# A hybrid decoder layer on one core: weight splits moved to the highest scheduling priority, a triangular inverse dealt in two halves, and recurrence states rewritten with fewer VectorE operations

## The chip, the core and the metric

The kernel runs on one core of a Trainium2 chip. Its time is the device time of one execution in microseconds (us). Five engines work beside each other, each through its own instructions in order: TensorE (PE: matmuls, with its weight loads shown as PEld), VectorE (DVE), ScalarE (ACT), GpSimd (POOL) and SyncE (SP, which issues most of the transfers). An engine that waits for another holds everything that is queued behind the waiting instruction.

## What is computed

The reference is one residual layer. The input is normalised and multiplied by one wide matrix; four token mixers work on slices of that product; each mixer's output is gated, projected and merged, and an output projection is added to the input.

```python
h = rmsnorm(x, norm_gain)
proj = h @ w_in
ys = (gated_deltanet(...), spatial_gating(...), rwkv7_time_mix(...), native_sparse_attention(...))
gates = jnp.split(jax.nn.sigmoid(merge), N_MIXERS, axis=-1)
mixed = gates[0] * (ys[0] @ w_branch[0])
for i in range(1, N_MIXERS):
    mixed = mixed + gates[i] * (ys[i] @ w_branch[i])
x = x + mixed @ w_out
```

Two mixers are recurrences over the 1024 tokens: the gated DeltaNet (gdn) and RWKV-7. Both are worked in chunks of 32 tokens, in which the dependence inside a chunk is a unit lower triangular 32x32 system, and a state of 64x64 per head goes from chunk to chunk.

## The kernel before, in words

`body` first normalises x and splits it into a high and a low part (`hh`, `hl`, matmul type fp32r), so that a product of full precision is three matmuls. Then comes a row of **column tiles**: `col_tile(c, evac)` (L1008) loads 128 columns of the weight matrix in two halves (`load_w`, L997), splits each half into `wh` (a cast on ACT, L1004) and `wl` (a subtraction on DVE, L1006), and makes 48 matmuls of 512 columns in groups of three: `wh` with `hh` (L1017), `wl` with `hh` (L1018), `wh` with `hl` (L1019). `wt`, `wh` and `wl` have three buffers each, so a split can only run when the matmuls of an older half are done.

The order of the program text is: column tiles for RWKV; `rwkv`; column tiles for gdn; `gdn`; column tiles for the sparse attention (`nsa`) and `nsa` itself; the spatial mixer (`gmlp`); 32 column tiles for the merge gates; the branch products (L1250 to L1252) and the output projection (L1281 to L1284). The engines don't run it in this order. A scheduler takes all instructions and, with its own estimate of durations, hands them to the engines' queues; among those that it holds to be ready, the one earlier in the program text goes first. So column tiles written after a mixer fill the mixer's waiting times on PE, and their splits come behind the mixer's own DVE and ACT work. Each queue is fixed before the program runs.

`rwkv` and `gdn` go over four quarters of 256 tokens. A quarter is prepared (convolution or token shift, decays, products of keys; in gdn L465 is the convolution, L478 writes `KQ`, L480 the values), its eight triangular systems per four heads are inverted, and then eight steps of the recurrence run.

`unit_lower_inverse` (L81) inverts 32 systems of 32x32 at once on DVE. The rows of the inverse are dealt over four groups of 32 partitions: a partition holds 8 of the 32 rows of one system, rows 8g to 8g+7 for group g. `X` is (128, 8, 32). It walks from the last column pair to the first: for each of 16 values of c it multiplies all 8 rows by two columns of `L` (L98, 16 x m elements, m = 32-c) and sums the products (L100). The 32 instructions form one chain. Two transposes on PE (L103) and 16 copies (L110, L112) put the result where the recurrence needs it (`xt`).

A step of the recurrence is a chain over three engines. In rwkv: `py` (L312, L314) -> `R` (L319 DVE, L320 ACT) -> `px` (L322) -> `sv` (L323, L324) -> `ps` (L327) -> new state `S` by two DVE operations of 128x64 (L329), with `Sg`, the decayed old state, made ahead by L301. In gdn: `py` (L560) -> `R` by two DVE operations of 64x64 (L568) -> `px` of 64 columns (L572) -> `sa` (L573, L574) -> `ps` (L576) -> new state by two DVE operations of 128x64 (L578). L542, L544, L287 and L288 make the outputs of the step before.

Of the kernel before, what the change touches and what calls it, by code (L numbers as in the profile page):

```python
# [10 lines left out]
F32 = mybir.dt.float32  # L11
# [21 lines left out]
def setup(tc, ctx):  # L33
# [19 lines left out]
    for g in range(4):  # L53
        nc.gpsimd.iota(inv0[32 * g:32 * g + 32], pattern=[[-1, 8], [1, 32]], base=-8 * g, channel_multiplier=0,
                       allow_small_or_imprecise_dtypes=True)
# [25 lines left out]
def unit_lower_inverse(G, pool, src, xt):  # L81


    nc = G.nc
# [11 lines left out]
    for c in range(30, -1, -2):  # L96
        m = 32 - c
        nc.vector.tensor_mul(prv[:, :, :, :m], X[:, :, None, c:].to_broadcast([128, 8, 2, m]),  # L98
                             L[:, None, c:c + 2, c:].to_broadcast([128, 8, 2, m]))
        nc.vector.tensor_reduce(X[:, :, c:c + 2], prv[:, :, :, :m], axis=AX.X, op=OP.add)  # L100
# [3 lines left out]
    for r in range(4):  # L104
        for h in range(4):
            a = pt[32 * r:32 * r + 32, 0:256].rearrange("c (k g n h) -> c h n g k", k=2, g=4, h=4)[:, h]
            d = xt[32 * h:32 * h + 32, :, 32 * h:32 * h + 32]
            d = d.rearrange("c n (g k r) -> c r n g k", g=4, k=2)[:, r]
            if h % 2:
                nc.scalar.copy(d, a)  # L110
            else:
                nc.vector.tensor_copy(d, a)  # L112
# [11 lines left out]
def rwkv(G, src, zs, y, up, cols):  # L124
# [3 lines left out]
    with tc.tile_pool(name="rw", bufs=1, reuse_waits="tile") as P:  # L128
# [29 lines left out]
        for q in range(4):  # L158
# [136 lines left out]
            for n in range(8):  # L295
# [4 lines left out]
                Sg = P.tile([128, 2, 64], F32, name="Sg", bufs=2)  # L300
                nc.vector.tensor_mul(Sg, S, gdec[:, :, n:n + 1].to_broadcast([128, 2, 64]))  # L301
# [26 lines left out]
                for p in range(2):  # L328
                    nc.vector.scalar_tensor_tensor(S2[:, p], ps[:, 64 * p:64 * p + 64], gdec[:, p, n:n + 1],  # L329
                                                   Sg[:, p], op0=OP.mult, op1=OP.add)  # L330
# [29 lines left out]
def gdn(G, src, small, zs, y, conv, hp, gnw):  # L360
# [3 lines left out]
    with tc.tile_pool(name="gd", bufs=1, reuse_waits="tile") as P:  # L364
# [85 lines left out]
        for q in range(4):  # L450
# [102 lines left out]
            for n in range(8):  # L553
# [11 lines left out]
                R = P.tile([128, 64], F32, name="gR", bufs=2)  # L565
                for p in range(2):
                    hs = slice(64 * p, 64 * p + 64)
                    nc.vector.scalar_tensor_tensor(R[hs], py[hs, hs], egc[hs, 1, nn:nn + 1], V[hs, n],  # L568
                                                   op0=OP.mult, op1=OP.add)
                px = sbank(G)  # L570
                sa = SA[n % 2]
                nc.tensor.matmul(px[:, :64], xt[:, n], R, start=True, stop=True)  # L572
                nc.vector.tensor_scalar(sa[0:64, 0:64], px[0:64, :64], cn[0:64, 0, n:n + 1], None, op0=OP.mult)  # L573
                nc.scalar.activation(sa[64:128, 64:128], px[64:128, :64], AF.Copy, scale=cn[64:128, 0, n:n + 1])  # L574
                ps = sbank(G)
                nc.tensor.matmul(ps[:, :128], TB[:, n], sa, start=True, stop=True)  # L576
                for p in range(2):
                    nc.vector.scalar_tensor_tensor(S2[:, p], S[:, p], gl[:, p, nn:nn + 1],  # L578
                                                   ps[:, 64 * p:64 * p + 64], op0=OP.mult, op1=OP.add)
# [401 lines left out]
def body(tc, xT, x, w, wsm, rw_up, rw_cols, gd_conv, gd_hp, gd_gw, gm_ws, gm_bs, gm_lg, gm_lb,  # L981
# [4 lines left out]
    with ExitStack() as ctx:  # L986
# [22 lines left out]
        def col_tile(c, evac):  # L1009
            parts = [split_w(load_w(w[c], 4 * kh, 128), nc.vector) for kh in range(2)]  # L1010
# [356 lines left out]
```

## Time and profile before

| | us |
|---|---|
| median of 3 runs (1254.69 to 1255.78) | 1254.97 |
| the profiled execution | 1258.43 |
| span of its trace | 1256.7 |
| PE busy (94%), 6214 matmuls | 1185.8 |
| DVE busy (68%), 2181 instructions | 849.0 |
| ACT busy (41%) | 519.6 |
| POOL busy (14%) | 175.2 |

The profiled execution is 3.5 us longer than the median, and 1.7 us of it lie outside the span. Times in the trace count from the span's start. The rwkv recurrence runs from about 200 to 400 us, gdn from about 500 to 705, and from 1050 to the last tile PE has next to no waits. An operation's row gives the time from its start to its end; of instructions that follow each other the next can start before the end of the one before.

### The profile page before, as it was taken

To read this page: it belongs to the slowest core of one execution; us is meant where nothing else is said; L and a number is where in the kernel's file an instruction comes from. 1 tells how busy PE (TensorE), PEld (TensorE's weight loads), DVE (VectorE), ACT (ScalarE), POOL (GpSimd) and SP (SyncE) were. 2 spreads that over 40 slices of the span, in tenths; PEclk is the share of its full clock that TensorE was granted. 3 is DMA by queue.
4 is the path that set the end of the run, shared out by engine and by line. 5 is a ranking of instruction groups with operands and counts; after the bars stand their busy time and mean duration, and the time that the engine had idled before them with its cause. 6 is when DMAs were issued, how large, how long until landed. Compare 5 with 4: busy or idle time off the path is not lost. (4 is left out here: it accounts for less than half of the span.)

```text
span 1256.7 us, 17997 instructions
## 1 busy us (share of the span) xinstructions
PE 1185.8 (94%) x6214; PEld 962.6 (77%) x6214; DVE 849.0 (68%) x2181; ACT 519.6 (41%) x1302; POOL 175.2 (14%) x158
## 2 busy tenths in 40 slices
PE   6999999898999997998999999999999799999997
PEld 6987777786777785776777778787877577888886
DVE  6612697878774677878795579989876833588222
ACT  5422553361433355363533355645555343221212
POOL 4320000000002000010100000000000320576510
PEclk9999999998999998999999999999999999999999
DMA  5222453122211444212322422121114275676323
GB/s 196 101 93 101 134 149 103 45 70 67 98 59 59 112 149 121 98 61 81 115 75 85 162 94 76 64 76 56 59 47 145 100 238 186 214 236 217 110 84 126
DMA packets 113103, 140.09 MB, mean 111 GB/s; under 512 B 36544, under 2 KB 59968, under 8 KB 112884
## 3 DMA queue, kind: packets, MB, share of 16 engines
q1 hardware_dynamic: 95588, 107.22, 27.2%
q10 hardware_dynamic: 17424, 31.73, 6.6%
q8 instruction: 49, 0.80, 0.3%
q14 instruction: 42, 0.34, 0.1%
HBM read 94.78 MB, written 44.12 MB: 111 GB/s over the span
## 5 line engine op out<-in xcount | busy, mean ns | idle before, releaser
L1018 PE MATMUL st<-hh,wl 128*128 128x512 f32 x944 | 384.5, 407 | 9.4 <-DVE wl L1006 9.4
L1017 PE MATMUL st<-hh,wh 128*128 128x512 f32 x944 | 381.9, 406 | 3.2 <-ACT stg L1045 2.0
L1019 PE MATMUL st<-hl,wh 128*128 128x512 f32 x944 | 381.3, 404 | 0.0
L1018 PEld LDWEIGHTS st<-hh,wl 128*128 128x128 f32 x944 | 180.8, 192 | 44.0 <-DVE wl L1006 10.9
L1017 PEld LDWEIGHTS st<-hh,wh 128*128 128x128 f32 x944 | 180.2, 191 | 38.0 <-ACT stg L1045 3.5
L1019 PEld LDWEIGHTS st<-hl,wh 128*128 128x128 f32 x944 | 180.9, 192 | 32.3 <-issue 0.8
L1006 DVE TENSOR_TENSOR wl<-wt,wh 128x512 fp32r<-128x512 f32 x134 | 99.3, 744 | 94.2 <-ACT wh L1004 91.7
L1004 ACT CAST wh<-wt 128x512 fp32r<-128x512 f32 x140 | 86.4, 619 | 80.8 <-PE st L1019 66.5
L1045 ACT ACTIVATE stg<-st 128x512 f32<-128x512 f32 x64 | 38.2, 596 | 77.3 <-PE st L1019 76.9
L98 DVE TENSOR_TENSOR invP<-invX,invL 128x32 f32<-128x32 f32 (+15 forms) x128 | 55.7, 435 | 1.7
L100 DVE TENSOR_REDUCE invX<-invP 128x16 f32<-128x32 f32 (+15 forms) x128 | 54.9, 429 | 1.8
L915 ACT ACTIVATE P<-sc,m 128x512 f32<-128x512 f32 (+3 forms) x80 | 44.7, 564 | 25.3 <-DVE m L913 11.6
L1281 PE MATMUL sc<-woh,hh 128*128 128x512 f32 x128 | 49.8, 389 | 0.0
L1282 PE MATMUL sc<-wol,hh 128*128 128x512 f32 x128 | 49.8, 389 | 0.0
L1287 DVE TENSOR_TENSOR o<-sc,xr 128x512 f32<-128x512 f32 x16 | 11.1, 691 | 56.1 <-PE sc L1284 56.1
L1028 ACT COPY stg<-st 128x512 f32<-128x512 f32 x39 | 23.1, 591 | 61.0 <-PE st L1019 57.6
L1258 POOL TENSOR_TENSOR mx<-mx,stg 128x512 f32<-128x512 f32 x28 | 38.6, 1379 | 47.7 <-DVE stg L1257 46.6
L910 DVE TENSOR_REDUCE m<-sc 128x1 f32<-128x512 f32 (+3 forms) x80 | 40.7, 528 | 0.9 <-PE sc L835 0.3
L1264 ACT CAST hh<-mx 128x512 fp32r<-128x512 f32 x16 | 9.9, 621 | 62.6 <-POOL mx L1258 54.8
L30 POOL IOTA tril<- 128x128 f32 x1 | 0.2, 248 | 237.4 <-PE sc L835 237.4
L588 POOL TENSOR_TENSOR gst<-gst,mhalf 128x8 f32<-128x8 f32 x4 | 6.7, 1678 | 190.6 <-DVE gst L587 190.6
L254 POOL MEMSET sv<- 64x512 f32 x8 | 4.2, 519 | 207.8 <-ACT O L292 165.3
(457 smaller groups left out, 2400.7 us busy)
## 6 DMA issues: line engine op xcount, KB each, us to landing
wt<-in_w_dram SPq DMA_DIRECT2D x124, 256.0 KB, 2.7
gate<-stg ACTq DMA_DIRECT2D x64, 256.0 KB, 2.1
gt<-gate SPq DMA_DIRECT2D x32, 256.0 KB, 3.4
stg<-gate SPq DMA_DIRECT2D x32, 256.0 KB, 3.0
xt<-in_xT_dram SPq DMA_DIRECT2D x8, 512.0 KB, 5.0
wot<-in_wo_dram SPq DMA_DIRECT2D x16, 256.0 KB, 3.7
wt<-in_wb_dram SPq DMA_DIRECT2D x16, 256.0 KB, 3.5
xr<-in_x_dram SPq DMA_DIRECT2D x16, 256.0 KB, 2.5
```

The lines of the kernel that those rows point to most:

```text
L98: nc.vector.tensor_mul(prv[:, :, :, :m], X[:, :, None, c:].to_broadcast([128, 8, 2, m]), L[:, None, c:c + 2, c:].to_broadcast([128, 8, 2, m]))
L100: nc.vector.tensor_reduce(X[:, :, c:c + 2], prv[:, :, :, :m], axis=AX.X, op=OP.add)
L910: nc.vector.tensor_reduce(m2[:, h, gi:gi + 1], pz[:, :n], axis=AX.X, op=OP.max, negate=True)
L915: nc.scalar.activation(Pt[gi][:, h, :n], pp[gi][:, :n], AF.Exp, bias=m2[:, h, 0:1], accum_out=ss[:, gi, h:h + 1])
L1004: nc.scalar.copy(wh, wt)
L1006: eng.tensor_sub(wl, wt, wh.bitcast(F32))
L1017: nc.tensor.matmul(p, wh[:, kk], hh[:, k, sl], start=(k == 0), stop=False)
L1018: nc.tensor.matmul(p, wl[:, kk], hh[:, k, sl], start=False, stop=False)
L1019: nc.tensor.matmul(p, wh[:, kk], hl[:, k, sl], start=False, stop=(k == 7))
L1258: (nc.vector if j == 7 else nc.gpsimd).tensor_add(mx, mx, g)
L1281: nc.tensor.matmul(p, mh[:, k, ts], a[:, k], start=(k == 0), stop=False)
L1282: nc.tensor.matmul(p, mh[:, k, ts], b[:, k], start=False, stop=False)
```

## The change

1. `col_tile` puts the two instructions of a split (cast on ACT, subtraction on DVE) under `tc.high_priority()`: whenever the scheduler holds them to be ready, they go before anything else. The load of the weights stays where it was.
2. `unit_lower_inverse` deals the rows in turn (row 4r+g in place r of group g), so that all groups have the same number of rows that are not yet known to be zero; for a given c only rows from r0 = c//4 on are worked, in two halves of rows with an instruction each. There are 60 instructions in place of 32, and 3,120 products and as many sums per partition in place of 4,352 (the sum of rows x 2 x m over all c).
3. rwkv: the new state is (`ps` + S) times the decay: an addition and a multiplication of 128x128, in place of `Sg` and the two operations of L329.
4. gdn: `Sg` (the decayed state) is made ahead by two ACT operations of 128x64; `R` is one DVE operation of 128x128 with both head pairs (the halves that are not needed come along); `px` has 128 columns in place of 64; the new state is one addition of 128x128.

```diff
 setup:
-        nc.gpsimd.iota(inv0[32 * g:32 * g + 32], pattern=[[-1, 8], [1, 32]], base=-8 * g, ...
+        nc.gpsimd.iota(inv0[32 * g:32 * g + 32], pattern=[[-4, 8], [1, 32]], base=-g, ...
 unit_lower_inverse:
     for c in range(30, -1, -2):
-        m = 32 - c
-        nc.vector.tensor_mul(prv[:, :, :, :m], X[:, :, None, c:].to_broadcast([128, 8, 2, m]),
-                             L[:, None, c:c + 2, c:].to_broadcast([128, 8, 2, m]))
-        nc.vector.tensor_reduce(X[:, :, c:c + 2], prv[:, :, :, :m], axis=AX.X, op=OP.add)
+        m, r0 = 32 - c, c // 4
+        halves = [slice(r0, (r0 + 8) // 2), slice((r0 + 8) // 2, 8)] if r0 < 7 else [slice(7, 8)]
+        for rs in halves:
+            d = [128, rs.stop - rs.start, 2, m]
+            nc.vector.tensor_mul(prv[:, rs, :, :m], X[:, rs, None, c:].to_broadcast(d),
+                                 L[:, None, c:c + 2, c:].to_broadcast(d))
+        for rs in halves:
+            nc.vector.tensor_reduce(X[:, rs, c:c + 2], prv[:, rs, :, :m], axis=AX.X, op=OP.add)
 rwkv:
-                Sg = P.tile([128, 2, 64], F32, name="Sg", bufs=2)
-                nc.vector.tensor_mul(Sg, S, gdec[:, :, n:n + 1].to_broadcast([128, 2, 64]))
...
-                for p in range(2):
-                    nc.vector.scalar_tensor_tensor(S2[:, p], ps[:, 64 * p:64 * p + 64], gdec[:, p, n:n + 1],
-                                                   Sg[:, p], op0=OP.mult, op1=OP.add)
+                Su = P.tile([128, 2, 64], F32, name="Sg", bufs=2)
+                nc.vector.tensor_add(Su, ps[:, 0:128].rearrange("q (p e) -> q p e", p=2), S)
+                nc.vector.tensor_mul(S2, Su, gdec[:, :, n:n + 1].to_broadcast([128, 2, 64]))
 gdn:
-                R = P.tile([128, 64], F32, name="gR", bufs=2)
+                Sg = P.tile([128, 2, 64], F32, name="gSg", bufs=2)
                 for p in range(2):
-                    hs = slice(64 * p, 64 * p + 64)
-                    nc.vector.scalar_tensor_tensor(R[hs], py[hs, hs], egc[hs, 1, nn:nn + 1], V[hs, n],
-                                                   op0=OP.mult, op1=OP.add)
+                    nc.scalar.activation(Sg[:, p], S[:, p], AF.Copy, scale=gl[:, p, nn:nn + 1])
+                R = P.tile([128, 2, 64], F32, name="gR", bufs=2)
+                nc.vector.scalar_tensor_tensor(R, py[:, :128].rearrange("q (p e) -> q p e", p=2), egc[:, 1, nn:nn + 1],
+                                               V[:, n, None, :].to_broadcast([128, 2, 64]), op0=OP.mult, op1=OP.add)
-                nc.tensor.matmul(px[:, :64], xt[:, n], R, start=True, stop=True)
+                nc.tensor.matmul(px[:, :128], xt[:, n], R.rearrange("q p e -> q (p e)"), start=True, stop=True)
-                for p in range(2):
-                    nc.vector.scalar_tensor_tensor(S2[:, p], S[:, p], gl[:, p, nn:nn + 1],
-                                                   ps[:, 64 * p:64 * p + 64], op0=OP.mult, op1=OP.add)
+                nc.vector.tensor_add(S2, ps[:, :128].rearrange("q (p e) -> q p e", p=2), Sg)
 col_tile:
-            parts = [split_w(load_w(w[c], 4 * kh, 128), nc.vector) for kh in range(2)]
+            parts = []
+            for kh in range(2):
+                wt = load_w(w[c], 4 * kh, 128)
+                with tc.high_priority():
+                    parts.append(split_w(wt, nc.vector))
```

The scheduler makes a new order of all queues from this. The first place is DVE's queue in gdn, in the second half of the first quarter's inverse (`invP` is the product, `invX` the inverse, `cvt` the convolution of a later quarter, `stg` a gate's evacuation). Before:

```order
L100 TENSOR_REDUCE invX<-invP 128x8x2
L465 SCALAR_TENSOR_TENSOR cvt<-graw,cw,cvt 128x256
L98 TENSOR_TENSOR invP<-invX,invL 128x16x24
L465 SCALAR_TENSOR_TENSOR cvt<-graw,cw,cvt 128x256
L100 TENSOR_REDUCE invX<-invP 128x8x2
L1038 SCALAR_TENSOR_TENSOR stg<-stg 128x512
L98 TENSOR_TENSOR invP<-invX,invL 128x16x26
L1038 SCALAR_TENSOR_TENSOR stg<-stg 128x512
L100 TENSOR_REDUCE invX<-invP 128x8x2
L480 SCALAR_TENSOR_TENSOR cvt<-gth,cvt 128x512
L98 TENSOR_TENSOR invP<-invX,invL 128x16x28
L1006 TENSOR_TENSOR wl<-wt,wh 128x512
```

With the change, at the same part of the inverse (L102 is the product, L105 the sum, L1008 the subtraction of a split):

```order
L102 TENSOR_TENSOR invP<-invX,invL 128x6x18
L102 TENSOR_TENSOR invP<-invX,invL 128x6x26
L105 TENSOR_REDUCE invX<-invP 128x3x2 x2
L1008 TENSOR_TENSOR wl<-wt,wh 128x512
L102 TENSOR_TENSOR invP<-invX,invL 128x6x20
L102 TENSOR_TENSOR invP<-invX,invL 128x6x28
L105 TENSOR_REDUCE invX<-invP 128x3x2 x2
L102 TENSOR_TENSOR invP<-invX,invL 128x6x22
L102 TENSOR_TENSOR invP<-invX,invL 128x8x30
L105 TENSOR_REDUCE invX<-invP 128x3x2
L105 TENSOR_REDUCE invX<-invP 128x4x2
L102 TENSOR_TENSOR invP<-invX,invL 128x6x24
```

Before, every instruction of the inverse has a convolution or another operation of other work behind it, and the split's `wl` comes after all of the convolution; now the inverse's two halves follow each other, a `wl` stands between them, and the third quarter's convolution starts only at the inverse's last steps.

The second place is PE's queue from the `ps` of one step of gdn to the `px` of the next (last quarter). Before (L576 is `ps`, L560 `py`, L572 `px`):

```order
L576 MATMUL sc<-gSA_3539,gTB 128x128
L1019 MATMUL st<-hl,wh 128x512
L1017 MATMUL st<-hh,wh 128x512
L1018 MATMUL st<-hh,wl 128x512
L1019 MATMUL st<-hl,wh 128x512
L560 MATMUL sc<-gS,KQ_3536 128x128
L542 MATMUL sc<-gS,KQ_3536 128x128
L544 MATMUL sc<-gSA_3539,gKK 128x128
L1017 MATMUL st<-hh,wh 128x512
L1018 MATMUL st<-hh,wl 128x512
L572 MATMUL sc<-gR,gXT_3538 128x64
```

With the change (L580 is `ps`, L563 `py`, L576 `px`, L1023 to L1025 the column tiles):

```order
L580 MATMUL sc<-gSA_3619,gTB 128x128
L1023 MATMUL st<-hh,wh 128x512
L1024 MATMUL st<-hh,wl 128x512
L1025 MATMUL st<-hl,wh 128x512
L563 MATMUL sc<-gS,KQ_3616 128x128
L545 MATMUL sc<-gS,KQ_3616 128x128
L547 MATMUL sc<-gSA_3619,gKK 128x128
L1023 MATMUL st<-hh,wh 128x512
L576 MATMUL sc<-gR,gXT_3618 128x128
```

Of column matmuls, four stood between `ps` and `py` and now three; two stood before `px` and now one. Those taken out stand further back in the queue.

## Rows read from the trace of the kernel before

**Rows 1.** gdn's stretch: busy us (count) of PE, PEld, DVE, ACT, POOL; PE's clock; DMA.

```profile
500.00:725.00 225.00, 210.59 (x1085) 166.13 (x1085) 166.35 (x499) 95.18 (x270) 11.35 (x11) 0.96 0.31 101
```

**Rows 2.** Waits of PE: who for whom, us in total, times, longest us.

```profile
PE st L1018 <- DVE wl L1006: 9.4, 3, 7.6
PE m L272 <- DVE AR L251: 7.0, 3, 3.6
PE m L681 <- DVE gmv L674: 4.7, 1, 4.7
PE m L488 <- DVE KQ L478: 4.4, 3, 2.1
```

**Rows 3.** Timeline, 479 to 506 us, of PE: start us, us, instruction [idle before].

```profile
479.84 1.97 PE L525 MATMUL m<-KQ 128*64 128x128 f32 x32
...
500.87 0.80 PE L1018 MATMUL st<-hh,wl 128*128 128x512 f32 x1 [7.65 <-DVE wl L1006]
...
505.73 0.63 PE L103 MATMUL sc<-ident,invX 128*128 128x128 f32 x2
```

**Rows 4.** Timeline of ACT: the cast of the same split.

```profile
492.55 0.63 ACT L1004 CAST wh<-wt 128x512 fp32r<-128x512 f32 x1
```

**Rows 5.** Timeline of DVE: the split's subtraction, start and end of the inverse.

```profile
480.85 0.18 DVE L98 TENSOR_TENSOR invP<-invX,invL 128x32 f32<-128x32 f32 x1
...
500.13 0.68 DVE L1006 TENSOR_TENSOR wl<-wt,wh 128x512 fp32r<-128x512 f32 x1
...
504.44 0.69 DVE L100 TENSOR_REDUCE invX<-invP 128x16 f32<-128x512 f32 x1
```

**Rows 6.** Stretch behind that wait, columns as in rows 1.

```profile
500.80:506.40 5.60, 5.53 (x15) 4.36 (x16) 4.26 (x9) 0.01 (x1) 0.00 (x0) 0.50 0.86 282
```

**Rows 7.** Page, groups: line, operation, count | busy us, mean ns | idle before.

```profile
L98 DVE TENSOR_TENSOR invP<-invX,invL 128x32 f32<-128x32 f32 (+15 forms) x128 | 55.7, 435 | 1.7
L100 DVE TENSOR_REDUCE invX<-invP 128x16 f32<-128x32 f32 (+15 forms) x128 | 54.9, 429 | 1.8
```

**Rows 8.** Groups by shape of the inverse's product, widest and narrowest.

```profile
L98 DVE TENSOR_TENSOR invP<-invX,invL 128x512 f32<-128x512 f32 x8 | 5.5, 689 | 0.2
...
L98 DVE TENSOR_TENSOR invP<-invX,invL 128x32 f32<-128x32 f32 x8 | 1.5, 185 | 0.1
```

**Rows 9.** Timeline of DVE: two operations that don't depend on each other.

```profile
485.09 0.32 DVE L98 TENSOR_TENSOR invP<-invX,invL 128x160 f32<-128x160 f32 x1
485.33 0.48 DVE L465 SCALAR_TENSOR_TENSOR cvt<-graw,cw,cvt 128x256 f32<-128x256 f32 x1
```

**Rows 10.** Groups by shape: the state operations, and one of 128x128 out of PSUM.

```profile
L568 DVE SCALAR_TENSOR_TENSOR gR<-sc,egc,gV 64x64 f32<-64x64 f32 x64 | 18.1, 283 | 8.3 <-PE sc L560 7.1
L907 DVE TENSOR_TENSOR sc<-sc,ndg 128x128 f32<-128x128 f32 x64 | 17.7, 293 | 8.4 <-PE sc L835 8.1
L329 DVE SCALAR_TENSOR_TENSOR S<-sc,gdec,Sg 128x64 f32<-128x64 f32 x64 | 15.2, 279 | 14.9 <-PE sc L327 14.5
L578 DVE SCALAR_TENSOR_TENSOR gS<-gS,gl,sc 128x64 f32<-128x64 f32 x64 | 15.0, 275 | 11.5 <-PE sc L576 11.3
L301 DVE TENSOR_TENSOR Sg<-S,gdec 128x128 f32<-128x128 f32 x32 | 9.2, 288 | 0.4
```

**Rows 11.** Groups: PE's matmuls of 64 and of 128 columns in gdn.

```profile
L560 PE MATMUL sc<-gS,KQ 128*128 128x128 f32 x64 | 13.3, 292 | 1.6 <-DVE gS L578 1.6
L572 PE MATMUL sc<-gR,gXT 128*128 128x64 f32 x64 | 12.4, 276 | 2.9 <-ACT gXT L110 2.5 <-DVE gR L568 0.3
```

**Rows 12.** Timeline of PE: 128-column matmuls back to back.

```profile
855.34 0.27 PE L946 MATMUL m<-ident,P 128*128 128x128 f32 x1
855.45 0.27 PE L946 MATMUL sc<-ident,P 128*128 128x128 f32 x1
```

**Rows 13.** Groups: ACT's widest operation in a step of gdn.

```profile
L547 ACT ACTIVATE gO<-sc,egc 128x128 f32<-128x128 f32 x32 | 11.7, 367 | 38.7 <-PE sc L544 38.5
```

**Rows 14.** Timeline of DVE: where `wl` held the queue in gdn's preparation.

```profile
453.32 0.69 DVE L1006 TENSOR_TENSOR wl<-wt,wh 128x512 fp32r<-128x512 f32 x1 [4.81 <-ACT wh L1004]
...
476.86 0.69 DVE L1006 TENSOR_TENSOR wl<-wt,wh 128x512 fp32r<-128x512 f32 x1 [5.00 <-ACT wh L1004]
```

More of the change, by code (lines that the diff above doesn't have):

```diff
@@ L53, in setup @@
     for g in range(4):
-        nc.gpsimd.iota(inv0[32 * g:32 * g + 32], pattern=[[-1, 8], [1, 32]], base=-8 * g, channel_multiplier=0,
+        nc.gpsimd.iota(inv0[32 * g:32 * g + 32], pattern=[[-4, 8], [1, 32]], base=-g, channel_multiplier=0,
                        allow_small_or_imprecise_dtypes=True)
@@ L107, in unit_lower_inverse @@
             d = xt[32 * h:32 * h + 32, :, 32 * h:32 * h + 32]
-            d = d.rearrange("c n (g k r) -> c r n g k", g=4, k=2)[:, r]
+            d = d.rearrange("c n (k r g) -> c r n g k", g=4, k=2)[:, r]
             if h % 2:
@@ L564, in gdn @@
                         last = outputs(n - 1, S0, sa)
-                R = P.tile([128, 64], F32, name="gR", bufs=2)
+                Sg = P.tile([128, 2, 64], F32, name="gSg", bufs=2)
                 for p in range(2):
-                    hs = slice(64 * p, 64 * p + 64)
-                    nc.vector.scalar_tensor_tensor(R[hs], py[hs, hs], egc[hs, 1, nn:nn + 1], V[hs, n],
-                                                   op0=OP.mult, op1=OP.add)
+                    nc.scalar.activation(Sg[:, p], S[:, p], AF.Copy, scale=gl[:, p, nn:nn + 1])
+                R = P.tile([128, 2, 64], F32, name="gR", bufs=2)
+                nc.vector.scalar_tensor_tensor(R, py[:, :128].rearrange("q (p e) -> q p e", p=2), egc[:, 1, nn:nn + 1],
+                                               V[:, n, None, :].to_broadcast([128, 2, 64]), op0=OP.mult, op1=OP.add)
                 px = sbank(G)
                 sa = SA[n % 2]
-                nc.tensor.matmul(px[:, :64], xt[:, n], R, start=True, stop=True)
-                nc.vector.tensor_scalar(sa[0:64, 0:64], px[0:64, :64], cn[0:64, 0, n:n + 1], None, op0=OP.mult)
-                nc.scalar.activation(sa[64:128, 64:128], px[64:128, :64], AF.Copy, scale=cn[64:128, 0, n:n + 1])
+                nc.tensor.matmul(px[:, :128], xt[:, n], R.rearrange("q p e -> q (p e)"), start=True, stop=True)
+                nc.vector.tensor_scalar(sa[0:64, 0:64], px[0:64, 0:64], cn[0:64, 0, n:n + 1], None, op0=OP.mult)
+                nc.scalar.activation(sa[64:128, 64:128], px[64:128, 64:128], AF.Copy, scale=cn[64:128, 0, n:n + 1])
                 ps = sbank(G)
                 nc.tensor.matmul(ps[:, :128], TB[:, n], sa, start=True, stop=True)
-                for p in range(2):
-                    nc.vector.scalar_tensor_tensor(S2[:, p], S[:, p], gl[:, p, nn:nn + 1],
-                                                   ps[:, 64 * p:64 * p + 64], op0=OP.mult, op1=OP.add)
+                nc.vector.tensor_add(S2, ps[:, :128].rearrange("q (p e) -> q p e", p=2), Sg)
                 S0, S = S, S2
```

## The prediction

> **What bounds the kernel now.** I read the page first, then the waits of PE, then the timeline around the longest of them, then the groups that price the edited instructions. The page shows PE busy for 94% of the span, so the kernel ends when PE has worked off its queue; time can only be won where PE stands still, runs at the lower clock, or does less. No edit takes a matmul away. So the question is which of PE's waits the change removes, and what it puts in their place.
>
> The waits of PE [rows 2] are few and short, and those I list all end with a DVE result: 9.4 us for the low part of a weight split, 7.0 for the inputs of rwkv's chunk products (L272), 4.7 for gmlp's normalised values (L681), 4.4 for gdn's keys (L488). In gdn's stretch [rows 1] DVE is busy for 166 of 225 us, and PE's granted clock is 0.96 on average. The clock has two levels, 1.2 and 2.4 GHz, so 0.96 means that about 8% of the stretch, 18 us, ran at the lower one; work done there takes twice as long, so some 9 us are lost.
>
> One wait makes up most of the 9.4 us. At 500.87 PE starts a column matmul after 7.65 us of idling [rows 3]; it waited for a `wl` that DVE began at 500.13 [rows 5]. The cast that `wl` needs had ended at 492.55 + 0.63 = 493.18 [rows 4]. The subtraction was late only because of its place in DVE's queue, behind convolutions and the inverse, as the first excerpt of the order shows. Behind the wait PE ran 5.6 us at the lower clock, granted clock 0.50 [rows 6].
>
> **The splits at the highest priority, with the inverse: -10 us.** The priority alone would give almost nothing here. The next thing that PE needs is the inverse, at L103. The inverse's last sum ends at 504.44 + 0.69 = 505.13 [rows 5], and PE started L103 at 505.73 [rows 3]. Without the wait on `wl` PE would stand at L103 instead, and 0.6 us would be won. That is the lower end. But the order now also keeps the convolution out of the inverse. Before, 32 instructions took from 480.85 to 505.13, 24.3 us [rows 5], while their own durations sum to (55.7 + 54.9) / 8 = 13.8 us [rows 7].
>
> The new inverse: a product of 512 elements takes 689 ns and one of 32 takes 185 [rows 8], which is 1.05 ns an element and 151 ns fixed. 60 instructions over 6,240 elements are 60 x 0.151 + 6,240 x 0.00105 = 9.1 + 6.6 = 15.6 us, if each waits for the end of the one before. Of two operations that don't depend on each other the second begins earlier: one that began at 485.09 and took 0.32, to 485.41, was followed at 485.33 [rows 9], 0.08 us before its end. The two halves don't depend on each other at once, so up to 60 x 0.08 = 4.8 us go: 10.8 us. From 480.85, with two `wl` of 0.68 between, the inverse ends between 493 and 498.
>
> PE took from 479.84 to 505.73 between L525 and L103 [rows 3]. Less 7.65 of waiting, and less half of the 5.6 us at the lower clock (2.8), it would come to L103 at 495.3, 10.4 us earlier. It then waits 0 to 2.8 us for the inverse. I take a gain of 9, as the order shows the halves paired almost throughout. The other two waits for `wl` are 9.4 - 7.65 = 1.75 us together; I take 1 of it. Ends of this term: -0.6 and -12.2.
>
> **A lighter DVE: -8 us.** The inverse gives DVE 13.8 - 10.8 = 3.0 us in each of 8 quarters, 24 us. In gdn a step's `R` costs 18.1 / 32 = 0.57 us and the state 15.0 / 32 = 0.47 [rows 10]. One operation of 128x128 out of PSUM takes 0.29, the row of L907 [rows 10]; `R` becomes one (up to 0.35, being one with a scalar and two inputs: 0.279 for 64 elements plus 64 x 1.05 ns), the state the other. That is 0.4 us a step, 12.7 in all. In rwkv the pair takes 15.2 / 32 = 0.475 and `Sg` 0.288; now an addition (0.293) and a multiplication (0.288) do it [rows 10], 0.18 us a step, 5.8 in all. DVE gets some 42 us back, all in the stages where PE waits for it. The waits it could shorten are 7.0 + 4.7 + 4.4 = 16.1 us [rows 2]. I take half, since the new order also lets PE arrive earlier at such places: the second excerpt has fewer column matmuls in a step. Ends: 0 and -16.1.
>
> **Work that is added.** `px` in gdn has 64 more columns in 64 passes. The group of 128 columns is busy 13.3 us against 12.4 for 64 columns [rows 11], +0.9; passes of 128 columns follow each other by 0.11 us [rows 12], and half of that for 64 passes is +3.5. I take +2. In rwkv the chain grows, as the multiplication must follow the addition: 0.293 + 0.288 against 0.475 is +0.106 us a step, 3.4 in all. Column matmuls in the step cover it in most steps; I take +1, ends 0 and +3.4. gdn's 64 new ACT operations cost at most 64 x 0.367 = 23.5 us of ACT [rows 13], which is busy 95 of 225 us there [rows 1]. They need only the old state and lie beside `py` and `R`; if they came in front of ACT's half of `sa`, up to all of it would go into the chain. I cost them at nothing. The shorter chain of gdn, 0.4 us a step less the wider `px`, I cost at nothing as well: the scheduler took column matmuls out of the step to fit, and PE does them later. The dealing of rows moves only patterns of `iota` and copies, in equal numbers.
>
> **Sum.** -10 - 8 + 2 + 1 = -15 us on the profiled execution of 1258.4, so 1243.4; that execution stands 3.5 us above the median, and on the median of 1255 it is **1240**. The forecast's own range is 1228 (every gain at its end, -27) to 1250 (a third of the sum).
>
> **Rivals.**
>
> *The wait only moves* (chance 0.13). PE leaves the split's wait and stands at the inverse, or at the recurrence's next result. For it: the inverse ended only 0.6 us before PE came [rows 3, 5]. Against it: the convolution has left the inverse. Then -0.6 + 3, and a quarter of the second term (-4): -1.6, 1253.
>
> *The splits hold DVE's queue* (0.14, slower). A split ahead of everything is handed out as soon as a buffer is expected to be free; where PE is late, the cast waits for PE, `wl` for the cast, and everything on DVE behind it. This happens already: `wl` held DVE for 4.81 and 5.00 us in gdn's preparation [rows 14], the second time right ahead of the inverse. If each of the 8 inverses gets one more such hold of 4.9 us and half reaches PE, +20; with -10 + 3 that is +13, 1268. It decides for slower once more than 15 us of new holds reach PE. Against it: in the same trace the casts were done well before their `wl` where DVE was full [rows 4, 5].
>
> *Twice the instructions* (0.06, slower). If the halves don't overlap, an inverse takes 15.6 us and not 13.8, the first term gives 7, the other seven inverses come 1.8 us later, 12.5, and the second term is gone: +8.5, 1263. Rows 9 speak against it, with their 0.08 us. The Trainium skill, VectorE: DVE Perf Modes, in The DRAIN you can't avoid and Rules for kernel authors, says that after each operation the next can't start until the pipe is empty, so the count of operations is to be kept small; by that rule the halves win nothing, and the time would be this rival's. The same page adds that an instruction that isn't held starts earlier; the trace agrees with that part.
>
> *More than the sum* (0.13). Every listed wait goes (-28) and, with fewer waits, half of the 9 us lost to the clock in gdn comes back: -32, 1223.
>
> The forecast keeps 0.54. About 0.2% (2.5 us) is what a measurement of this kernel can tell from no change. Faster than that: 0.54 + 0.13 = 0.67; within: 0.13; slower: 0.20. The range of 1221 to 1262 takes in the larger gain and the moved wait, and leaves out the queue's holds and little else.
>
> **What would show it.** Right: no wait of PE on `wl` above 2 us near 490 to 510; the inverse groups sum to about 125 us of durations, but a first gdn inverse lasts under 17 us from first to last; L103 is reached some 9 us earlier; granted clock in gdn above 0.96. Wrong: new waits of PE at L103, `px` or `py` of 5 us and more; idle time of DVE ahead of `wl` with the inverse behind it; inverse operations that follow each other by their full duration.

## The result, and the profile after

| | us, median (lowest to highest) | span of the profiled execution | mean granted clock |
|---|---|---|---|
| before, in the same runs | 1255.89 (1254.69 to 1257.62) | 1256.7 | 0.977 |
| with the change | 1226.2 (1225.36 to 1229.06) | 1223.6 | 0.995 |

The ratio is 0.9768, with a 95% interval of 0.9755 to 0.9781. The change gains 29.7 us. The forecast of 1240 had the direction, and its range of 1221 to 1262 holds the time, but the gain is twice the 15 us that it expected.

First the page of the changed kernel: busy time of each engine, share of the span and number of instructions, and the three column matmuls of a split (line, operation, count | busy us, mean ns | idle just before).

```profile
PE 1168.8 (96%) x6214; PEld 948.3 (78%) x6214; DVE 816.5 (67%) x2309; ACT 539.0 (44%) x1366; POOL 176.8 (14%) x158
...
L1023 PE MATMUL st<-hh,wh 128*128 128x512 f32 x944 | 380.4, 403 | 2.3 <-ACT stg L1051 2.3
L1024 PE MATMUL st<-hh,wl 128*128 128x512 f32 x944 | 379.4, 402 | 0.0
L1025 PE MATMUL st<-hl,wh 128*128 128x512 f32 x944 | 377.2, 400 | 0.0
```

PE executes the same 6214 matmuls. Its busy time fell from 1185.8 us (94% of 1256.7) to 1168.8, by 17.0, and the rest of its span from 70.9 to 54.8, by 16.1. Of the 33.1 us between the two profiled spans, half is thus PE standing still less, and half is PE taking less time over the same work. The second half is the clock. With two levels of 1.2 and 2.4 GHz, a mean of 0.977 says that 4.6% of the span, some 58 us, ran at the lower one; 0.995 leaves some 12 us. L1024, the matmul that reads `wl`, waits for nothing now; before it stood 9.4 us [rows 2].

The waits of PE, with the columns of rows 2:

```profile
PE st L1117 <- ACT wh L1006: 6.5, 1, 6.5
PE m L491 <- DVE KQ L481: 4.4, 3, 2.2
PE sc L108 <- DVE invX L105: 4.3, 4, 1.8
PE m L683 <- DVE gmv L676: 3.6, 2, 1.9
```

The first is the program's start and stood in the kernel before with the same 6.5 us. No wait is above 2.2 us besides. `KQ` is unchanged from rows 2, `gmv` is 1.1 less, and the wait for `AR` of 7.0 has left the head of the list. The wait for the inverse at L108 is new, 4.3 us in four pieces.

Busy time by stretch, with the columns of rows 1: rwkv, gdn's preparation and gdn's recurrence. First the two stretches before that rows 1 leave out, then all three with the change.

```profile
200.00:425.00 225.00, 209.46 (x1167) 171.55 (x1165) 158.91 (x481) 86.79 (x261) 15.79 (x19) 0.96 0.25 75
425.00:500.00 75.00, 66.41 (x345) 52.24 (x345) 57.08 (x145) 40.96 (x133) 4.58 (x3) 0.95 0.38 114
```

```profile
200.00:425.00 225.00, 212.99 (x1220) 172.46 (x1219) 162.94 (x561) 92.96 (x270) 15.55 (x19) 1.00 0.25 74
425.00:500.00 75.00, 72.96 (x404) 58.45 (x403) 59.64 (x202) 45.98 (x153) 4.27 (x3) 1.00 0.46 145
500.00:725.00 225.00, 214.81 (x1275) 171.65 (x1274) 166.12 (x588) 121.90 (x365) 11.42 (x11) 0.99 0.31 100
```

In the last stretch PE starts 1275 matmuls where it started 1085 [rows 1], at a clock of 0.99 in place of 0.96. VectorE is as busy there as it was, 166 us: what the edits save is filled with work that used to come later.

What PE loses in a stretch can be estimated from these rows: its idle time, plus the length times what the clock lacks to 1.00. Before, that is 15.5 + 0.04 x 225 = 24.5 us in rwkv, 8.6 + 0.05 x 75 = 12.4 in gdn's preparation and 14.4 + 0.04 x 225 = 23.4 in its recurrence. With the change it is 12.0, 2.0 and 12.4. The rows give the clock in hundredths, which leaves each long stretch open by 1 us. By this estimate some 12 us of the gain lie in rwkv, 10 in the preparation and 11 in gdn's recurrence.

The first inverse of gdn on the timeline, of VectorE first and then of PE (start us, us, instruction):

```profile
459.32 0.34 DVE L102 TENSOR_TENSOR invP<-invX,invL 128x4 f32<-128x4 f32 x3
...
467.05 0.69 DVE L1008 TENSOR_TENSOR wl<-wt,wh 128x512 fp32r<-128x512 f32 x1 [0.58 <-ACT wh L1006]
...
475.71 0.42 DVE L105 TENSOR_REDUCE invX<-invP 128x8 f32<-128x256 f32 x1
```

```profile
463.72 1.97 PE L528 MATMUL m<-KQ 128*64 128x128 f32 x32
...
475.99 0.39 PE L1025 MATMUL st<-hl,wh 128*128 128x512 f32 x1
476.21 0.30 PE L108 MATMUL sc<-ident,invX 128*128 128x128 f32 x1
```

The inverse lasts from 459.32 to 476.13, 16.8 us against 24.3 [rows 5]. Two `wl` stand inside it. The one shown follows its cast at once, for which it held the queue 0.58 us; before, the `wl` that PE waited for came 7 us after its cast [rows 4, 5]. PE runs column matmuls back to back until the inverse is there, and needs 12.5 us from L528 to L108, with 44 column matmuls between, where it took 25.9 from L525 to L103 [rows 3], with 55.

### The profile page after: what moved, and what is told of

It is laid out like the page before. It is cut to its first block, busy times and chain, and to the rows that moved or that the text cites. A ratio compares the mean times of both kernels' runs of the same rounds, so it can differ in the third digit from the quotient of the medians.

```text
span 1223.6 us, 18178 instructions
## 1 busy us (share of the span) xinstructions
PE 1168.8 (96%) x6214; PEld 948.3 (78%) x6214; DVE 816.5 (67%) x2309; ACT 539.0 (44%) x1366; POOL 176.8 (14%) x158
## 5 line engine op out<-in xcount | busy, mean ns | idle before, releaser
L1023 PE MATMUL st<-hh,wh 128*128 128x512 f32 x944 | 380.4, 403 | 2.3 <-ACT stg L1051 2.3
L1024 PE MATMUL st<-hh,wl 128*128 128x512 f32 x944 | 379.4, 402 | 0.0
L1025 PE MATMUL st<-hl,wh 128*128 128x512 f32 x944 | 377.2, 400 | 0.0
L1023 PEld LDWEIGHTS st<-hh,wh 128*128 128x128 f32 x944 | 178.7, 189 | 35.9 <-ACT stg L1051 3.6
L1025 PEld LDWEIGHTS st<-hl,wh 128*128 128x128 f32 x944 | 178.4, 189 | 32.7 <-issue 1.0
L1024 PEld LDWEIGHTS st<-hh,wl 128*128 128x128 f32 x944 | 178.5, 189 | 32.3 <-issue 1.9
L1008 DVE TENSOR_TENSOR wl<-wt,wh 128x512 fp32r<-128x512 f32 x134 | 99.0, 740 | 96.4 <-ACT wh L1006 94.3
L102 DVE TENSOR_TENSOR invP<-invX,invL 128x16 f32<-128x16 f32 (+18 forms) x240 | 53.9, 259 | 0.3
L105 DVE TENSOR_REDUCE invX<-invP 128x8 f32<-128x240 f32 (+18 forms) x240 | 52.7, 252 | 0.2
L1293 DVE TENSOR_TENSOR o<-sc,xr 128x512 f32<-128x512 f32 x16 | 11.1, 692 | 56.1 <-PE sc L1290 56.1
L1270 ACT CAST hh<-mx 128x512 fp32r<-128x512 f32 x16 | 9.9, 622 | 62.6 <-POOL mx L1264 54.8
L1295 ACT ACTIVATE jk<-o 128x512 f32<-128x512 f32 x16 | 10.1, 631 | 51.6 <-DVE o L1293 51.6
```

Of the source, the lines that this page charges most:

```text
L102: nc.vector.tensor_mul(prv[:, rs, :, :m], X[:, rs, None, c:].to_broadcast(d), L[:, None, c:c + 2, c:].to_broadcast(d))
L105: nc.vector.tensor_reduce(X[:, rs, c:c + 2], prv[:, rs, :, :m], axis=AX.X, op=OP.add)
L1023: nc.tensor.matmul(p, wh[:, kk], hh[:, k, sl], start=(k == 0), stop=False)
L1024: nc.tensor.matmul(p, wl[:, kk], hh[:, k, sl], start=False, stop=False)
L1025: nc.tensor.matmul(p, wh[:, kk], hl[:, k, sl], start=False, stop=(k == 7))
```

## The experiments

Each kernel was timed in turn with the kernel before on the same chip; ratios are to that one. In all of them the computation is the reference's, in full.

**The parts alone.** The priority alone: only `col_tile` is changed.

```diff
-            parts = [split_w(load_w(w[c], 4 * kh, 128), nc.vector) for kh in range(2)]
+            parts = []
+            for kh in range(2):
+                wt = load_w(w[c], 4 * kh, 128)
+                with tc.high_priority():
+                    parts.append(split_w(wt, nc.vector))
```

> The kernel before with the highest priority for the weight splits alone. Theory (priority and inverse need each other): PE's 7.65 us wait on wl near 500 goes, but PE then stands at L103 for the inverse, so little is won there; 1250 to 1256 us. Rival 1 (the priority alone is the gain, as PE always has column matmuls at hand): 1230 or less. Rival 2 (splits hold DVE's queue): over 1260, with new idle time of DVE ahead of wl.

Measured: 1236.05 us, ratio 0.9826 (0.9805 to 0.9847), -21 us: between the theory and the first rival, and nearer to the rival. The sentence "the priority alone would give almost nothing here" has fallen. PE's waits in this kernel, and its stretch of rwkv:

```profile
PE sc L103 <- DVE invX L100: 8.2, 2, 6.7
...
PE m L272 <- DVE AR L251: 2.3, 2, 2.0
```

```profile
200.00:425.00 225.00, 213.88 (x1222) 175.65 (x1221) 160.67 (x485) 90.34 (x266) 15.60 (x19) 1.00 0.28 79
```

At the place that the forecast looked at it was right: the wait of 7.65 us on `wl` has become one of 6.7 at L103. The gain lies elsewhere. In rwkv, where PE had not waited for a `wl` at all (its waits on `wl` of rows 2 lie behind 500 us), the granted clock is 1.00, and PE does 1222 matmuls in the 225 us; before, it did 1167 at a clock of 0.96. By the estimate of idle time and clock, some 13 us come back in rwkv, 9 in gdn's preparation (idle 3.1 us, clock 1.00) and 6 in its recurrence (13.2 us, 0.98). The fall of the wait at L272, from 7.0 to 2.3, is not due to the priority in particular: with the inverse alone, the slowest of these kernels, it is 0.9, and with the states alone it is gone.

The new inverse alone: the `iota` pattern, the halves and the copies of `unit_lower_inverse`, with the splits in their old place.

```diff
...
-        m = 32 - c
-        nc.vector.tensor_mul(prv[:, :, :, :m], ...
...
+        m, r0 = 32 - c, c // 4
+        halves = [slice(r0, (r0 + 8) // 2), slice((r0 + 8) // 2, 8)] if r0 < 7 else [slice(7, 8)]
+        for rs in halves:
...
+            nc.vector.tensor_mul(prv[:, rs, :, :m], ...
```

> The kernel before with the dealt inverse in two halves alone. Theory (a lighter DVE ahead of PE's hand-offs): the first gdn inverse gets shorter, DVE wins up to 24 us, but a wait on wl is left where convolutions stand ahead of it; 1240 to 1250 us. Rival 1 (the priority is all of the gain): 1254 to 1258. Rival 2 (twice the instructions cost more than the elements save): 1258 to 1264.

Measured: 1289.67 us, ratio 1.0251 (1.0226 to 1.0275), 32 us slower and outside all three expectations, although VectorE's busy time fell from 849.0 to 838.0 us. This was the run that taught most. On the timeline of VectorE and then of ScalarE, around the third inverse (265.56 to 286.64):

```profile
264.85 0.65 DVE L1011 TENSOR_TENSOR wl<-wt,wh 128x512 fp32r<-128x512 f32 x1
...
313.98 0.67 DVE L1011 TENSOR_TENSOR wl<-wt,wh 128x512 fp32r<-128x512 f32 x1
```

```profile
278.95 0.62 ACT L1009 CAST wh<-wt 128x512 fp32r<-128x512 f32 x1 [0.94 <-PE st L1024]
...
282.63 0.63 ACT L1009 CAST wh<-wt 128x512 fp32r<-128x512 f32 x1
```

The casts are done at 279.57 and 283.26; the next `wl` follows at 313.98, 34 us behind the first. In the whole inverse there is none. Counted on the timeline, as each `wl` that begins between an inverse's first product and its last sum, five of the eight inverses of this kernel have no split inside them, the others one or two; in the kernel before each has one to four. PE in the stretch behind, first of this kernel and then of the one with the priority alone (columns as in rows 1):

```profile
285.00:318.00 33.00, 23.69 (x132) 19.84 (x131) 26.59 (x71) 11.01 (x36) 0.00 (x0) 0.69 0.19 60
```

```profile
285.00:318.00 33.00, 31.01 (x172) 24.94 (x170) 28.33 (x64) 10.57 (x27) 2.75 (x3) 1.00 0.27 88
```

Without split weights no column matmul on `wl` runs in these 33 us (none, against 32 with the priority; the kernel before, at the same times, has 26 and a clock of 0.84). PE has a single column matmul there besides the recurrence and its preparation, stands between the steps, and the clock is at its lower level for much of the stretch. This is how the wait on a split costs: only part of it is named `wl`, since the scheduler has put the column matmuls later in PE's queue as well, and the rest of the list are the chain's own waits, which nothing covers. PE's longest waits in this kernel:

```profile
PE sc L108 <- DVE invX L105: 12.8, 6, 2.9
PE st L1023 <- DVE wl L1011: 11.4, 5, 4.5
PE m L493 <- DVE KQ L483: 9.4, 2, 6.9
PE sc L577 <- ACT gXT L115: 6.7, 4, 4.4
```

The same inverse with the priority (the kernel with the old states, below) differs from this one by the place of the splits alone:

```profile
PE sc L108 <- DVE invX L105: 8.0, 6, 1.9
...
PE m L493 <- DVE KQ L483: 2.8, 4, 2.1
PE sc L577 <- ACT gXT L115: 2.7, 4, 0.8
...
PE st L1027 <- DVE wl L1011: 0.3, 1, 0.3
```

Between the two, PE's idle time falls from 90.8 to 55.3 us. Of these 35.5 us, 11.1 bear the name `wl`.

The states alone: the edits in the recurrences of rwkv and gdn, of which the core is

```diff
-                Sg = P.tile([128, 2, 64], F32, name="Sg", bufs=2)
-                nc.vector.tensor_mul(Sg, S, gdec[:, :, n:n + 1].to_broadcast([128, 2, 64]))
...
+                nc.vector.tensor_add(Su, ps[:, 0:128].rearrange("q (p e) -> q p e", p=2), S)
+                nc.vector.tensor_mul(S2, Su, gdec[:, :, n:n + 1].to_broadcast([128, 2, 64]))
...
+                nc.vector.tensor_add(S2, ps[:, :128].rearrange("q (p e) -> q p e", p=2), Sg)
```

> The kernel before with the new state operations of rwkv and gdn alone. Theory: they take some 18 us from DVE and shorten gdn's steps, but PE's column matmuls cover the steps; 1248 to 1256 us. Rival (the recurrences' chain is what PE waits for in small pieces): 1240 or less, with the clock in gdn's stretch near 0.99.

Measured: 1242.79 us, ratio 0.9884 (0.9866 to 0.9902), -15 us: between the theory and the rival. Its stretches of rwkv and of gdn's recurrence:

```profile
200.00:425.00 225.00, 207.64 (x1165) 167.59 (x1164) 159.04 (x465) 90.75 (x272) 15.16 (x19) 0.96 0.25 72
```

```profile
500.00:725.00 225.00, 214.95 (x1281) 172.27 (x1280) 167.41 (x505) 121.94 (x365) 12.55 (x11) 0.99 0.30 97
```

In rwkv nothing is gained (1165 matmuls at a clock of 0.96, before 1167 at 0.96). In gdn's recurrence there are 1281 matmuls for 1085, at a clock of 0.99 as the rival had it; by the estimate of idle time and clock this stretch holds 11 of the 15 us.

A control, meant to give every queue a new order at no other change: one copy in the inverse goes to another engine.

```diff
-    nc.scalar.copy(X, G.inv0)
+    nc.gpsimd.tensor_copy(X, G.inv0)
```

> A control: the kernel before with the eight copies that set X to the identity's rows moved from ScalarE to GpSimd, which does no work less but gives the scheduler another start. Theory (the edits' gain has causes that the trace names): within 5 us of before. Rival (any new order of the queues moves the time by the size of the gain): more than 10 us away from before, in either direction.

Measured: 1257.66 us, ratio 1.0002 (0.9991 to 1.0012). But it did not give a new order where it counts: in its trace all 6214 matmuls of PE and all 2181 instructions of VectorE run in the same sequence as before, and only the copies moved. So this run shows that moving the copies costs nothing. It does not test the rival: how far an arbitrary new order would move the time is shown by no run here, while each of the parts gives these queues an order of its own (with the priority alone, 2261 of PE's 6214 matmuls stand where they stood).

**The whole change with one part undone.** The splits back in their old place:

```diff
...
-                with tc.high_priority():
-                    parts.append(split_w(wt, nc.vector))
+            parts = [split_w(load_w(w[c], 4 * kh, 128), nc.vector) for kh in range(2)]
```

> The change without the priority: dealt inverse in halves and lighter states, splits in their old place. Theory 'pushed out': the halves fill each other's gaps, so that an inverse lasts some 17 us and not 26 and no weight split gets in between (with the inverse alone: 0 to 3 of them, before 1 to 7); the column matmuls then wait for `wl`. Then the time is above that of the kernel before, 1258 to 1275 us, with PE waits on `wl` of 8 us and more and the granted clock under 0.98. Rival 'DVE was too full': the inverse alone was slow because DVE had no room, and the lighter states give it room: 1225 to 1240 us. Effects that simply add (31.5 of the inverse, -14.6 of the states, on 1257.4): 1274 us.

Measured: 1266.69 us, ratio 1.0081 (1.0066 to 1.0097), clock 0.973, and 5.7 us of PE's waits on `wl`. Slower than before, as 'pushed out' had it, though its waits on `wl` are less than the 8 us expected, in seven pieces. Five of its eight inverses have no split inside them again; the counts in the expectation, up to 7 and up to 3, are higher than those of the trace.

The inverse as before, with its `iota` and its copies:

```diff
-        for rs in halves:
-            nc.vector.tensor_mul(prv[:, rs, :, :m], ...
+        nc.vector.tensor_mul(prv[:, :, :, :m], ...
```

> The change without the new inverse: priority and lighter states. Theory 'pushed out': with the priority the splits stand ahead of the inverse whatever its form, so the new inverse is worth only what it takes from DVE and from the waits at the product with the inverse: this run 1227 to 1234 us, slower than the whole change by 1 to 8. Rival 'effects add': -21.9 and -14.6 on 1257.4 give 1221 us, faster than the whole change, and the new inverse is a loss in any company.

Measured: 1234.17 us, ratio 0.9823 (0.9806 to 0.9839). 'Effects add' is refuted. Beside the priority the new inverse is a gain: from 0.9823 to 0.9768, 7 us, and the intervals don't meet. The run also tells of the states: priority with states is at 0.9823 and the priority alone at 0.9826, so without the new inverse the states gave nothing once the priority was there. What they gave alone lies in gdn's recurrence (above), and the priority alone wins time there too (1220 matmuls for 1085, clock 0.98), so the two gains overlap and do not add. Which step of the chain the states freed was not settled.

The states as before, in rwkv and gdn:

```diff
-                nc.vector.tensor_add(Su, ps[:, 0:128].rearrange("q (p e) -> q p e", p=2), S)
-                nc.vector.tensor_mul(S2, Su, gdec[:, :, n:n + 1].to_broadcast([128, 2, 64]))
+                for p in range(2):
+                    nc.vector.scalar_tensor_tensor(S2[:, p], ...
```

> Priority and new inverse, states as before. Theory 'pushed out': the priority takes away what made the inverse alone slow: 1230 to 1238 us, with no PE wait on `wl` above 1 us and the granted clock at 0.99; the difference to the whole change is then the states' part, 4 to 12 us. Rival 'effects add': -21.9 and +31.5 on 1257.4 give 1267 us.

Measured: 1230.12 us, ratio 0.9790 (0.9773 to 0.9806), clock 0.993, and a single PE wait on `wl`, of 0.3 us. The priority turns the inverse from a loss of 32 us into a gain of some 5 over the priority alone, with intervals that just overlap. The states' share, 0.9790 to 0.9768, is 3 us with intervals that overlap: below what was expected, and not resolved.

The dealt rows, but each step of the inverse in one operation:

```diff
-        halves = [slice(r0, (r0 + 8) // 2), slice((r0 + 8) // 2, 8)] if r0 < 7 else [slice(7, 8)]
+        halves = [slice(r0, 8)]
```

> The whole change, but each step of the inverse in one piece: the dealt rows still leave out what is zero, 32 operations in place of 60, which depend on each other in a row. By the groups' durations (150 ns fixed, 1.05 ns an element) an inverse has 32 x 0.15 + 6.5 = 11.4 us of own work, against 15.3 in halves. Theory 'the halves matter for latency': the inverse gets gaps again, others fill them, it lasts 22 us and more, PE waits for it at the product by 3 us more: 1228 to 1234 us. Rival 'fewer instructions' (32 us of DVE time less over 8 inverses, and splits are first anyway): 1218 to 1225 us.

Measured: 1233.32 us, ratio 0.9817 (0.9797 to 0.9838), 7 us slower than the whole change though VectorE has 224 instructions less. Its busy time is only 3.4 us less (813.1 against 816.5), not the 32 of the expectation, because the halves of the whole change overlap. Two products of 416 ns each, as one row of the whole change's timeline:

```profile
470.64 0.70 DVE L102 TENSOR_TENSOR invP<-invX,invL 128x256 f32<-128x256 f32 x2
```

The first gdn inverse lasts 22.8 us again, with 28 other VectorE operations begun in it (16.8 with 12 in the whole change). But PE's waits for `invX`, expected 3 us longer, have all but gone, and the granted clock is 0.98 in both recurrences (1.00 and 0.99 in the whole change). So the 7 us are not the wait for the halves' own product. What they are was not found, and a mere effect of the new order is not excluded.

**Where in VectorE's queue.** The inverse alone again, with only the split's subtraction raised:

```diff
-            eng.tensor_sub(wl, wt, wh.bitcast(F32))
+            with (tc.high_priority() if first else ExitStack()):
+                eng.tensor_sub(wl, wt, wh.bitcast(F32))
...
```

> The new inverse alone (1289.7 us with the splits in their old place), with the highest priority for a column split's subtraction on VectorE only; its cast on ScalarE stays where it was. With both at the highest priority this kernel took 1230.1 us. Theory 'pushed out of VectorE's queue': the subtraction's place is what counts, 1228 to 1242 us, and a split or more stands inside nearly every inverse again. Rival 'the cast's place counts': little comes back, 1260 to 1290 us, with PE waiting for `wl` and VectorE for the cast as before. In between, both count in the proportion of the times.

Measured: 1244.43 us, ratio 0.9898 (0.9881 to 0.9916), between the two ranges. Two or three splits stand in every inverse again. Of the way from 1.0251 to 0.9790 the subtraction's place on VectorE makes (1.0251 - 0.9898) / (1.0251 - 0.9790) = 77%; the rest needs the cast on ScalarE to be raised too. The rest is seen in rwkv, where this kernel is no better than the one before (1159 matmuls, clock 0.95; with the cast raised as well 1207 and 0.98), while in gdn's recurrence it has 1258 matmuls at 0.99.

**Splits off VectorE.** The same question by other means: the subtraction of the column splits on GpSimd, in the kernel before and with the inverse alone.

```diff
-            parts = [split_w(load_w(w[c], 4 * kh, 128), nc.vector) for kh in range(2)]
+            parts = [split_w(load_w(w[c], 4 * kh, 128)) for kh in range(2)]
```

> The kernel before, with the subtraction of every column split moved from VectorE to GpSimd (1.3 us each there in the start of the trace, against 0.69). Nothing else is changed, no priority. Theory 'pushed out' (the column matmuls are late because their `wl` stands in VectorE's queue behind other work): it acts like the priority, 1228 to 1240 us, with little waiting of PE on `wl`. Rival 'it is the order of the cast and the loads that the priority changes, not VectorE's queue': 1252 to 1262 us.

> The new inverse alone, again with the column splits' subtraction on GpSimd and no priority. With the splits on VectorE the new inverse alone cost 31.5 us. Theory 'pushed out': an inverse without gaps can't push out a split that isn't in its queue, so that loss goes: within 8 us of the kernel before with splits on GpSimd, to either side. Rival 'the inverse in 60 instructions is slow by itself, or late for its own product': 20 us and more above that kernel.

Measured: 1276.18 us, ratio 1.0155 (1.0132 to 1.0178), and 1285.57, ratio 1.0230 (1.0203 to 1.0256). Neither theory has the first of these; the edit brought a cost of its own. VectorE's groups in the first (line, operation, count | busy us, mean ns | idle before), and two of them in the kernel before:

```profile
L98 DVE TENSOR_TENSOR invP<-invX,invL 128x32 f32<-128x32 f32 (+15 forms) x128 | 66.0, 515 | 1.8
L100 DVE TENSOR_REDUCE invX<-invP 128x16 f32<-128x32 f32 (+15 forms) x128 | 55.0, 430 | 2.1
...
L465 DVE SCALAR_TENSOR_TENSOR cvt<-graw,cw,cvt 128x256 f32<-128x256 f32 x72 | 40.6, 597 | 0.2
L923 DVE TENSOR_SCALAR P<-P,ss 128x384 f32<-128x384 f32 (+3 forms) x80 | 33.0, 473 | 0.1
...
L568 DVE SCALAR_TENSOR_TENSOR gR<-sc,egc,gV 64x64 f32<-64x64 f32 x64 | 18.1, 282 | 9.6 <-PE sc L560 8.8
```

```profile
L465 DVE SCALAR_TENSOR_TENSOR cvt<-graw,cw,cvt 128x256 f32<-128x256 f32 x72 | 32.1, 476 | 0.1
L923 DVE TENSOR_SCALAR P<-P,ss 128x384 f32<-128x384 f32 (+3 forms) x80 | 27.2, 403 | 0.1
```

The product of two tensors in SBUF rose from 435 ns [rows 7] to 515 and the convolution from 476 to 597; the reduction of one tensor (429 to 430) and `gR`, which reads PSUM (283 to 282, [rows 10]), did not. One operation on a single tensor in SBUF, a TENSOR_SCALAR at L923, did rise, from 403 to 473. On the timeline one convolution beside a GpSimd subtraction takes 1.35 us. VectorE's busy time is 839.2 us, though 118 subtractions of at least 0.66 us, 78 us together, have left its 849.0: some 68 us went to operations that got longer. The Trainium skill, GPSIMD Engine Reference, section 1. Specifications, says that GpSimd shares its SBUF interfaces with VectorE and contends with its instructions that have two SBUF inputs or run in a 2-port mode; the trace agrees for the former, and can't show in which mode L923 ran. So the first run doesn't test the theory, though PE's waits on `wl` are 1.4 us in it, as the theory had it. The second, against the first, bears on it with that cost in both: the new inverse costs 9 us there and 32 with the splits on VectorE. That is just outside the band of 8, and far from the rival's 20. PE's waits for the inverse are 13.4 us in the second and 6.7 in the first, so some of the 9 may be the rival's lateness.

**One buffer more** for each half of a split, in the whole change:

```diff
-        def split_w(wt, eng=nc.gpsimd, pool=sp, bufs=3):
+        def split_w(wt, eng=nc.gpsimd, pool=sp, bufs=4):
```

> The whole change with four buffers in place of three for each half of a split, so that a cast waits less for PE to free one (103.8 us of ACT's idling in the whole change) and `wl` less for its cast (94.3 us of VectorE's). Theory 'VectorE has room now, its holds cost nothing': 1222 to 1230 us, no difference. Rival 'the holds of VectorE's queue still cost' (the forecast's second rival, in a small form): 1212 to 1221 us.

Measured: 1228.66 us, ratio 0.9782 (0.9763 to 0.9801): no difference from the whole change. VectorE's holds at `wl` stay (97.2 us, 94.3 with three buffers), so the run doesn't tell what they cost; it tells that a third buffer is enough. None of the kernels tried beats the whole change.

## Why the prediction was right or wrong

| | priority as before | highest priority |
|---|---|---|
| inverse and states as before | 1 | 0.9826 |
| new inverse | 1.0251 | 0.9790 |
| new states | 0.9884 | 0.9823 |
| both | 1.0081 | 0.9768 |

All eight combinations of the three parts were run, so each part can be read in four companies (the ratios times 1256 us). The priority gains in all four: 22 and 58 us without the new states, 8 and 39 with them, the larger figure each time beside the new inverse. The new inverse loses 32 and 25 us without the priority and gains 4.5 and 7 with it. The new states gain 15 and 21 us without the priority, none and 3 with it. That the signs hold in orders which all differ speaks against chance; for a difference of 3 to 7 us, an effect of the order alone is not excluded.

*The splits at the highest priority, with the inverse, -10 us.* This term failed by its size and by its split. "The priority alone would give almost nothing here" was worked out from one wait and then used for the whole kernel; alone it gave 21 us. The step that failed is taking the list of PE's waits for the price of a late split. Before, 54 of the 134 splits' subtractions on VectorE began between 200 and 700 us, with the priority alone 58; with the inverse alone 47, and its time is the longest. PE is in order and the splits' column matmuls are what it does between the steps of a recurrence. Where they come late, it pays in waits that bear other names (with the new inverse, 24.4 of 35.5 us of idle time) and in clock (0.963 for 0.993).

*The clock.* The sum had 2.8 us of it, half of rows 6. Over the kernel it gave up to half of the 58 - 12 = 46 us that left the lower level, 23 us; by PE's busy time it was 17, with the wider `px` inside. This is most of the gap between 15 and 30. The forecast saw 9 us lost in gdn's stretch [rows 1] and did not count them, or rwkv's, into its likeliest case. The idle part was sized well as a sum: 7.2 us of the first term are left without its 2.8 of clock, with 8 of the second and less 3 of added work that is 12; measured 16. On the list, the waits for `wl` and `AR` gave 9.4 and 6.7, and the new one at L108 took 4.3 back.

*The inverse.* Its working holds where it speaks of VectorE. The widest halves take 416 and 412 ns, 151 + 256 x 1.05 = 420 by rows 8. The inverse groups sum to 240 x 0.259 + 240 x 0.252 = 122.6 us of durations, expected about 125; the first gdn inverse lasts 16.8 us, expected under 17. It does not hold for what VectorE gets back: 24 us were expected of the inverse, but its busy time fell by 11.0 with the inverse alone (849.0 to 838.0). What the working missed is that gaps in a chain had a use: the old inverse let one to four splits through, the new one few or none unless they are raised. What fills a gap made the part cost 32 us or gain some 5.

*A lighter DVE, -8 us.* Priority with both, against the priority alone, is 0.9826 to 0.9768, 7 us. The size holds, but its source doesn't: VectorE got 32.5 us back where 42 were expected, 20.7 of it by the states alone (849.0 to 828.3, expected 18.5). Nor does the division, since without the priority the states gave 15 and the inverse lost 32, and beside the priority the states alone gave nothing.

*Work that is added.* `px` of 128 columns is busy 13.4 us, 12.4 before [rows 11]: +1.0, inside 0.9 to 3.5. `R` takes 348 ns as one operation (forecast up to 0.35), the states 290, and gdn's new ACT operations 341 each, 19.3 us; PE's wait on ACT's half of `sa` (L580) is 2.2 us in four pieces, and its wait for rwkv's new state 0.4, where +1 was taken. Nothing here was mispriced by much.

*The rivals.* "More than the sum", 1223, came nearest to 1226.2, but its number is partly luck. It had 28 us of waits and 4.5 of clock; measured were 16 and 17, and the waits for `KQ` (4.4) and `gmv` (3.6) stayed. That fewer waits give the clock back was right. "The wait only moves" was true of its one place and wrong of the time. "The splits hold DVE's queue" did not happen with the change: VectorE's idling at `wl` is 94.3 us against 91.7. It grew with the inverse alone, to 137.0 us, where no priority had been given. "Twice the instructions" fell: the version with fewer instructions (one piece) is 7 us slower, and saves VectorE only 3.4 us. The rule of the Trainium skill behind that rival (VectorE: DVE Perf Modes, Rules for kernel authors), to keep the count of operations small, gives the wrong sign for these two.

## What to carry to other kernels

Where PE is in order and fills a recurrence's pauses with independent matmuls, the preparation of their operands goes ahead of everything on its engines: its lateness shows as other waits and as a lower clock, so read the granted clock by stretch and price its whole deficit, not the list of waits alone. Before a chain is made denser, ask what used to run in its gaps and who waits for that. Test parts of a change in company as well as alone: here one part cost 2.5% by itself and gained 0.5% beside the other two. And before a control is trusted to stand for a new order of the queues, compare the order in its trace with the one before.

## What was not expected of the hardware

A subtraction on GpSimd slows VectorE's operations with two SBUF inputs, by 18% in the mean for the inverse's products (435 to 515 ns) and 25% for the convolution (476 to 597), in a trace where GpSimd is busy 27% of the span; a TENSOR_SCALAR of one SBUF tensor lost 17% as well (403 to 473); the reduction of one tensor (429 to 430) and operations that read PSUM (`gR`, 283 to 282) kept their time.
